# Two pairs of sum banks per layer norm, and half of the last scaling moved to VectorE, in a two-block transformer kernel

## The chip, the cores and the metric

The kernel runs on one core of one Trainium2 chip. The metric is the device time of one execution in microseconds (us). TensorE (PE) does the matmuls, VectorE (DVE) and ScalarE (ACT) the elementwise work, GpSimd (POOL) a few subtractions, and SyncE (SP) issues the DMAs. Each engine works through its own list of instructions in the built program, and waits at one until the results that it needs are there.

## The reference

The model has two blocks over 512 tokens of width 1024. The first (adaptive norm, neighbourhood attention, a spatial gate, a mixture of experts) is not touched by the change. The second has two layers of FFN, mixer, FFN, and each of these six phases ends in a layer norm over the features:

```python
def _layernorm_2(x, g, b):
    xf = x.astype(jnp.float32)
    mu = jnp.mean(xf, axis=-1, keepdims=True)
    var = jnp.mean(jnp.square(xf - mu), axis=-1, keepdims=True)
    return ((xf - mu) * lax.rsqrt(var + LN_EPS)).astype(x.dtype) * g + b

for l in range(DEPTH_2):
    h = 0.5 * _swiglu(x, ffn_w_gate[l, 0], ffn_w_up[l, 0], ffn_w_down[l, 0])
    x = _layernorm_2(ALPHA * x + h, ln_g[l, 0], ln_b[l, 0])
    h = _mixer(x, ...)
    x = _layernorm_2(ALPHA * x + h, ln_g[l, 1], ln_b[l, 1])
    h = 0.5 * _swiglu(x, ffn_w_gate[l, 1], ffn_w_up[l, 1], ffn_w_down[l, 1])
    x = _layernorm_2(ALPHA * x + h, ln_g[l, 2], ln_b[l, 2])
```

## The kernel before, in words

**Layout.** The activations lie transposed: 128 partitions by 8 feature tiles (`d`, 0 to 7) by 512 tokens. Every matmul of the second block is done as three (`mm3`, lines 194 to 196): weights and activations are split into a high part (`wh`, `xh`) and a rest (`wl`, `xl`), and the products high by rest, rest by high and high by high are added in one PSUM bank.

**The six phases.** `second` (line 1483) runs FFN, mixer, FFN, FFN, mixer, FFN; here they and their norms are numbered 1 to 6. Eight PSUM banks are shared out once: six under the tag `any`, two under the tag `yo0`, which only the mixer's output uses. An FFN's output tile is called `y`, a mixer's `yo`; `ft` is the first thing that a phase computes (`first_tiles`, line 1139): four output tiles from the whole input, tokens 0 to 255 first and then tokens 256 to 511, 96 matmuls of 256 columns for each half. `t` is what an FFN computes after them.

**The norm.** The last output tile of an FFN, and the last four of a mixer, are computed in two halves of 256 tokens, so that the norm of the first half can run while TensorE still works on the second. For each tile, `Norm.sums` (line 1080) adds the residual (`x<-x,y`, L1083, VectorE), adds into `S` (L1088, VectorE), squares into `q` (L1090, ScalarE) and adds `q` into `Q` (L1091, VectorE). `Norm.finish` (line 1093) then runs once for each half: `token_stats` (line 1128) sums `S` and `Q` over the partitions by two matmuls with a matrix of ones, into the banks `pS` and `pQ`; ScalarE takes the mean (`mu<-pS`, L1133); VectorE and ScalarE make the variance (L1134, L1135) and its inverse root (L226, L209 to L212), which is written back into `pQ`. For each feature tile VectorE then subtracts the mean (L1117, which reads `pS`) and multiplies by the root (L1118, which reads `pQ`), ScalarE scales and shifts into `x` (L1119) and `xh` (L1124), and GpSimd makes `xl` (L1125). The `ft` matmuls of the next phase read `xh` and `xl`.

**The last norm** has no next phase: ScalarE's L1119 is the last step, and each of its results goes out by a DMA that SyncE issues (L1121). For its second half the mean is subtracted ahead of time (L1108) and VectorE only multiplies (L1115).

**What sets the order.** The kernel is written in one sequence, and a scheduler gives each engine its list when the program is built. A block under `high_priority(offset=150)` is treated as if it had been written 150 instructions earlier, as far as its inputs and its buffers allow; the sums and statistics of the second half of every norm are under it. Both halves of a norm used the same two banks `pS` and `pQ`, so the scheduler had to place the second half's two matmuls behind the first half's L1117 and L1118, which read those banks.

Of the kernel before, what the change touches and what calls it, by code (L numbers as in the profile page):

```python
# [10 lines left out]
AF = mybir.ActivationFunctionType  # L11
OP = mybir.AluOpType
# [17 lines left out]
HALVES = (slice(0, 256), slice(256, 512))  # L30
# [211 lines left out]
def at(xs, k):  # L242
    return xs[k // 4][:, k % 4]
# [79 lines left out]
def first_attention(c, x, cst, v_dram, sums_dram, ada_dram):  # L323

    nc, tc, a = c.nc, c.tc, c.a
    with ExitStack() as st:
# [49 lines left out]
        def heads(w, xh, xl, n, gain, done):  # L376

            ps = [c.ps("ph") for _ in range(2)]
            for k in range(KD):
                for mm in range(2):  # L380
                    c.mm3(ps[mm][:, :n], *w.cols((mm * 8 + k) * P, P), xh(k), xl(k), k == 0, k == 7)
            finish()
            sq = [c.t("hsq") for _ in range(2)]
            for mm in range(2):
                nc.scalar.square(sq[mm][:, :n], ps[mm][:, :n])
            late.append((ps, sq, n, gain, done))
# [40 lines left out]
        for i in range(4):  # L427
            v = c.t("v")
            nc.scalar.copy(v, own(w, i))
            finish()  # L430
            nc.gpsimd.dma_start(v_dram[i * P:(i + 1) * P, :], v)
# [637 lines left out]
class Norm:  # L1069
# [23 lines left out]
    def finish(self, sl):  # L1093
        c, nc, x = self.c, self.c.nc, self.x
        last = self.nxt is None
        steps = []
        if self.out is None:
            self.mu, self.var, self.ps = c.t("mu"), c.t("var"), (c.ps("pS"), c.ps("pQ"))
            self.out = (c.new_xs("xh"), c.new_xs("xl")) if not last else ()
            if not last:  # L1100
                self.w, steps = c.first_chunks(self.nxt, self.early)
        mu, total, rs = self.mu[:, sl], self.ps[0][:, sl], self.ps[1][:, sl]
        with c.tc.high_priority(offset=150 if sl == HALVES[1] else 0):
            token_stats(c, self.S[:, sl], self.Q[:, sl], D, mu, self.var[:, sl], rs, total, rs)
        g, b = (c.v2[:, o + self.col * KD:] for o in (V_LNG, V_LNB))
        if last and sl == HALVES[1]:
            for d in range(KD):
                nc.vector.tensor_sub(x[:, d, sl], x[:, d, sl], mu)  # L1108
        for d in range(KD):
            if steps and d >= 2 * (self.early - 1) and d % 2 == 0:  # L1110
                steps.pop(0)()
            t = c.t("n")[:, sl]
            r = x[:, d, sl]
            if last and sl == HALVES[1]:
                nc.vector.tensor_mul(t, r, rs)  # L1115
            else:
                nc.vector.scalar_tensor_tensor(t, total, -1.0 / D, r, op0=OP.mult, op1=OP.add)  # L1117
                nc.vector.tensor_mul(t, t, rs)  # L1118
            nc.scalar.activation(r, t, AF.Identity, bias=b[:, d:d + 1], scale=g[:, d:d + 1])  # L1119
            if last:  # L1120
                nc.sync.dma_start(c.a["o"][:, d, sl], r)  # L1121
            else:
                h = at(self.out[0], d)[:, sl]
                nc.scalar.activation(h, t, AF.Identity, bias=b[:, d:d + 1], scale=g[:, d:d + 1])  # L1124
                nc.gpsimd.tensor_sub(at(self.out[1], d)[:, sl], r, h.bitcast(F32))  # L1125


def token_stats(c, s, q, n, mu, var, rs, pS, pQ):

    nc = c.nc  # L1130
    nc.tensor.matmul(pS, c.ones, s, start=True, stop=True)
    nc.tensor.matmul(pQ, c.ones, q, start=True, stop=True)
    nc.scalar.mul(mu, pS, 1.0 / n)  # L1133
    nc.vector.tensor_mul(var, mu, mu)  # L1134
    nc.vector.scalar_tensor_tensor(var, pQ, 1.0 / n, var, op0=OP.mult, op1=OP.subtract)  # L1135
    c.rstd(rs, var, 1, 1e-5)
# [488 lines left out]
```

## Time and profile before

| | us |
|---|---|
| time, median of 3 executions | 2525.66 (2525.14 to 2526.16) |
| time of the profiled execution | 2528.47 |
| span of its trace, first to last instruction | 2526.7 |
| TensorE busy | 2417.3 |
| VectorE busy | 1380.8 |
| ScalarE busy | 1070.5 |
| GpSimd busy | 151.7 |
| mean granted TensorE clock | 0.983 |

The profiled execution is 2.81 us above the median, and its trace covers all of it but 1.8 us. Busy times are sums over the span; matmuls overlap one another, and their ends are modelled, so the distance between the starts of neighbouring matmuls tells more than their lengths. In a timeline the columns are the start, the length from the first to the last of a group, the engine, the line, the operation, output<-inputs, the shape and the count; in brackets stands the idle time of the engine just before, and what ended it.

### The profile page before, as it was taken

Reading aid. Unit: us, or ns where it says so; the run is one execution under the profiler, and the core shown is the slowest. Engines: PE = TensorE matmul, PEld = TensorE weight load, DVE = VectorE, ACT = ScalarE, POOL = GpSimd, SP = SyncE. Lnnn points to the kernel's source line nnn. Section 1 sums busy time; section 2 is a strip of 40 time slices with the busy share of each in tenths; the row PEclk is TensorE's granted clock in tenths of the full one; section 3 lists DMA queues with packets and bytes.
Section 4 is the critical chain, followed back from the end, with each engine's and each line's share of the span. In section 5 each row is a group of like instructions: output and inputs, shape, how many; then the busy total and the mean of one; then the engine's idle time right before and its main releaser. Section 6 shows DMA issues by size and latency. Waiting matters only on the chain.

```text
span 2526.7 us, 30984 instructions
## 1 busy us (share of the span) xinstructions
PE 2417.3 (96%) x12289; PEld 1997.4 (79%) x12289; DVE 1380.8 (55%) x2299; ACT 1070.5 (42%) x1646; POOL 151.7 (6%) x187
## 2 busy tenths in 40 slices
PE   7998869999999999998999999999999999999997
PEld 4785558888798888886888888888888867888886
DVE  4836569999733333489833333533333798433334
ACT  4426427888532232356632222522222555522223
POOL 0011101121000000010100000100000200100000
PEclk9999879999999999999999999999999999999999
DMA  7145759999522222321132222222223211222231
GB/s 284 71 125 194 293 218 351 388 394 391 200 82 98 88 94 92 118 100 51 51 109 91 101 92 92 101 100 93 91 95 105 105 67 51 100 88 96 92 98 61
DMA packets 59652, 348.11 MB, mean 138 GB/s; under 512 B 8832, under 2 KB 11104, under 8 KB 23408
## 3 DMA queue, kind: packets, MB, share of 16 engines
q1 hardware_dynamic: 47776, 311.45, 33.5%
q0 software_dynamic: 10576, 32.00, 4.3%
q10 hardware_dynamic: 1152, 2.66, 0.3%
q8 instruction: 97, 1.59, 0.3%
q14 instruction: 51, 0.42, 0.0%
HBM read 329.73 MB, written 16.33 MB: 137 GB/s over the span
## 4 chain that ended last, share of the span: by engine, by line
PE 69%; DVE 7%; issue 5%; ACT 3%; DMA 0%; POOL 0%; SPq 0%; ACTq 0%; another core or an unknown queue 0%; POOLq 0%; DVEq 0%
PE t L194 12%; PE t L195 12%; PE t L196 12%; PE y L194 6%; PE y L196 6%; PE y L195 6%; PE e L194 2%; PE e L196 2%; PE e L195 2%; DVE acc L1256 2%; PE ft L195 1%; PE ft L196 1%; PE ft L194 1%; ACT x L1119 1%; DVE wl L186 1%
## 5 line engine op out<-in xcount | busy, mean ns | idle before, releaser
L185 ACT CAST wh<-raw 128x1024 fp32r<-128x1024 f32 (+1 forms) x504 | 521.5, 1038 | 1069.5 <-PE t L196 364.4
L186 DVE TENSOR_TENSOR wl<-raw,wh 128x1024 fp32r<-128x1024 f32 (+1 forms) x504 | 600.5, 1205 | 624.8 <-ACT wh L185 621.0
L194 PE MATMUL t<-xh,wl 128*128 128x512 f32 x1440 | 561.5, 390 | 0.0
L195 PE MATMUL t<-xl,wh 128*128 128x512 f32 x1440 | 560.6, 389 | 0.0
L196 PE MATMUL t<-xh,wh 128*128 128x512 f32 x1440 | 560.3, 389 | 0.0
L194 PEld LDWEIGHTS t<-xh,wl 128*128 128x128 f32 x1440 | 270.3, 188 | 58.2 <-issue 2.3
L195 PEld LDWEIGHTS t<-xl,wh 128*128 128x128 f32 x1440 | 270.4, 188 | 56.4 <-issue 0.8
L196 PEld LDWEIGHTS t<-xh,wh 128*128 128x128 f32 x1440 | 270.3, 188 | 56.2
L194 PE MATMUL y<-hh,wl 128*128 128x512 f32 (+1 forms) x792 | 289.8, 366 | 2.1 <-DVE x L1083 2.1
L195 PE MATMUL y<-hl,wh 128*128 128x512 f32 (+1 forms) x792 | 290.2, 366 | 0.0
L196 PE MATMUL y<-hh,wh 128*128 128x512 f32 (+1 forms) x792 | 289.4, 365 | 0.0
L1169 DVE SCALAR_TENSOR_TENSOR s<-s,t 128x512 f32<-128x512 f32 x80 | 55.0, 687 | 255.5 <-PE t L196 255.5
L194 PEld LDWEIGHTS y<-hh,wl 128*128 128x128 f32 x792 | 149.3, 189 | 27.1 <-DVE x L1083 2.9
L195 PEld LDWEIGHTS y<-hl,wh 128*128 128x128 f32 x792 | 149.4, 189 | 24.4
L196 PEld LDWEIGHTS y<-hh,wh 128*128 128x128 f32 x792 | 149.4, 189 | 23.9
L1125 POOL TENSOR_TENSOR xl<-x,xh 128x256 fp32r<-128x256 f32 x80 | 62.9, 789 | 1423.6 <-ACT xh L1124 1422.2
L195 PE MATMUL ft<-xl,wh 128*128 128x256 f32 x384 | 109.7, 288 | 3.4 <-POOL xl L1125 3.4
L194 PE MATMUL ft<-xh,wl 128*128 128x256 f32 x384 | 106.0, 286 | 4.8 <-ACT xh L1124 4.8
L194 PE MATMUL e<-wh,hTl 128*128 128x512 f32 x272 | 108.6, 399 | 0.5 <-DVE hTl L186 0.5
L196 PE MATMUL ft<-xh,wh 128*128 128x256 f32 x384 | 108.3, 285 | 0.0
L196 PE MATMUL e<-wh,hTh 128*128 128x512 f32 x272 | 106.9, 393 | 0.0
L195 PE MATMUL e<-wl,hTh 128*128 128x512 f32 x272 | 106.6, 392 | 0.0
(471 smaller groups left out, 3420.4 us busy)
## 6 DMA issues: line engine op xcount, KB each, us to landing
raw<-in_w_gu SPq DMA_DIRECT2D x88, 1024.0 KB, 4.8
raw<-in_w SPq DMA_DIRECT2D x82, 1024.0 KB, 12.0
raw<-in_w_d SPq DMA_DIRECT2D x32, 1024.0 KB, 5.0
raw<-in_w_ada SPq DMA_DIRECT2D x24, 1024.0 KB, 6.7
pair<-in_w SPq DMA_DIRECT2D x14, 1024.0 KB, 11.1
raw<-in_w_in SPq DMA_DIRECT2D x14, 1024.0 KB, 4.8
raw<-in_w_out SPq DMA_DIRECT2D x12, 1024.0 KB, 4.7
raw<-in_w_d SPq DMA_DIRECT2D x32, 384.0 KB, 3.1
```

Source lines behind the costliest of these rows:

```text
L185: self.nc.scalar.copy(h, x)
L186: self.nc.vector.tensor_sub(l, x, h.bitcast(F32))
L194: mm(ps, al, bh, start=first, stop=False)
L195: mm(ps, ah, bl, start=False, stop=False)
L196: mm(ps, ah, bh, start=False, stop=last)
L1119: nc.scalar.activation(r, t, AF.Identity, bias=b[:, d:d + 1], scale=g[:, d:d + 1])
L1125: nc.gpsimd.tensor_sub(at(self.out[1], d)[:, sl], r, h.bitcast(F32))
L1169: nc.vector.scalar_tensor_tensor(s, s, 0.5, ps[1], op0=OP.mult, op1=OP.mult)
L1256: nc.vector.scalar_tensor_tensor(acc[:, t], yp[:, t, j:j + S], w, acc[:, t], op0=OP.mult, op1=OP.add)
```

## The change

Two things change, both in `Norm.finish`. The two sums of a half are no longer slices of one shared pair of banks: the first half takes two banks of the tag `yo0`, the second half takes `pS` and `pQ` from the tag `any`. And in the second half of the last norm the scaling of the odd feature tiles is a VectorE instruction in place of a ScalarE one.

```diff
         if self.out is None:
-            self.mu, self.var, self.ps = c.t("mu"), c.t("var"), (c.ps("pS"), c.ps("pQ"))
+            self.mu, self.var = c.t("mu"), c.t("var")
...
-        mu, total, rs = self.mu[:, sl], self.ps[0][:, sl], self.ps[1][:, sl]
+        mu = self.mu[:, sl]
+        total, rs = (c.ps("yo0" if sl == HALVES[0] else n)[:, sl] for n in ("pS", "pQ"))
         with c.tc.high_priority(offset=150 if sl == HALVES[1] else 0):
             token_stats(c, self.S[:, sl], self.Q[:, sl], D, mu, self.var[:, sl], rs, total, rs)
...
-            nc.scalar.activation(r, t, AF.Identity, bias=b[:, d:d + 1], scale=g[:, d:d + 1])
+            if last and sl == HALVES[1] and d % 2:
+                nc.vector.tensor_scalar(r, t, g[:, d:d + 1], b[:, d:d + 1], op0=OP.mult, op1=OP.add)
+            else:
+                nc.scalar.activation(r, t, AF.Identity, bias=b[:, d:d + 1], scale=g[:, d:d + 1])
```

Line numbers shift: L1108, L1115, L1117 and L1118 become L1109, L1116, L1118 and L1119; from L1119 on it is four (L1119 becomes L1123, L1124 becomes L1128, and the statistics L1131 to L1135 become L1135 to L1139). L1121 is now the new VectorE instruction.

The scheduler makes new lists from this. **First place: TensorE at the end of phase 1**, where the second half's sums stand among the matmuls of phase 2. Before, `pS` came after 32 of the `ft` matmuls and `pQ` after 37 of the 192:

```order
L194 MATMUL ft<-xh,wl 128x256
L195 MATMUL ft<-xl,wh 128x256
L1131 MATMUL pS<-S,consts 128x256
L196 MATMUL ft<-xh,wh 128x256
L194 MATMUL ft<-xh,wl 128x256
L195 MATMUL ft<-xl,wh 128x256
L196 MATMUL ft<-xh,wh 128x256
L194 MATMUL ft<-xh,wl 128x256
L1132 MATMUL pQ<-Q,consts 128x256
L195 MATMUL ft<-xl,wh 128x256
```

and now:

```order
L194 MATMUL y<-hh_6469,wl 128x256
L195 MATMUL y<-hl_6491,wh 128x256
L196 MATMUL y<-hh_6469,wh 128x256
L1135 MATMUL pS<-S,consts 128x256
L1136 MATMUL pQ<-Q,consts 128x256
L194 MATMUL ft<-xh,wl 128x256
L195 MATMUL ft<-xl,wh 128x256
L196 MATMUL ft<-xh,wh 128x256
```

Both sums moved up to just behind the last `y` matmul, ahead of every `ft`. It is the same at the ends of phases 2 to 5, where `pQ` had stood behind 67, 53, 37 and 67 of the `ft` matmuls. At the end of phase 6 there is no `ft`, and TensorE's order is unchanged.

**Second place: VectorE and ScalarE at the same norm**, between the second half's `S` and its `Q`. VectorE before (`n` is the tile being normed, of the first half; `wl` the rest of a weight chunk):

```order
L1088 TENSOR_TENSOR S<-S,x_6300 128x256
L1118 TENSOR_TENSOR n<-n,pQ 128x256
L1117 SCALAR_TENSOR_TENSOR n<-pS,x_6300 128x256 x2
L1118 TENSOR_TENSOR n<-n,pQ 128x256
L186 TENSOR_TENSOR wl<-raw,wh 128x1024
L1118 TENSOR_TENSOR n<-n,pQ 128x256
L1117 SCALAR_TENSOR_TENSOR n<-pS,x_6300 128x256 x2
L1118 TENSOR_TENSOR n<-n,pQ 128x256
L1091 TENSOR_TENSOR Q<-Q,q 128x256
```

and now, with ScalarE's piece behind it:

```order
L1088 TENSOR_TENSOR S<-S,x_6300 128x256
L1119 TENSOR_TENSOR n<-n,yo_8717 128x256
L1118 SCALAR_TENSOR_TENSOR n<-yo_8716,x_6300 128x256 x2
L1119 TENSOR_TENSOR n<-n,yo_8717 128x256
L186 TENSOR_TENSOR wl<-raw,wh 128x1024
L1138 TENSOR_TENSOR var<-mu 128x256
L1119 TENSOR_TENSOR n<-n,yo_8717 128x256
L1118 SCALAR_TENSOR_TENSOR n<-yo_8716,x_6300 128x256 x2
L1119 TENSOR_TENSOR n<-n,yo_8717 128x256
L1091 TENSOR_TENSOR Q<-Q,q 128x256
```

```order
L185 CAST wh<-raw 128x1024
L1137 ACTIVATE mu<-pS 128x256
L1123 ACTIVATE x_6300<-n,vecs_85 128x256
L1128 ACTIVATE xh<-n,vecs_85 128x256
L1123 ACTIVATE x_6300<-n,vecs_85 128x256
L1128 ACTIVATE xh<-n,vecs_85 128x256
L1123 ACTIVATE x_6300<-n,vecs_85 128x256
L1090 ACTIVATE q<-x_6300 128x256
```

On VectorE `var<-mu` of the second half moved up, ahead of `Q`; on ScalarE `mu<-pS` moved up: it had stood behind `q` with two instructions between, and now stands ahead of `q` with five between. `Q` kept its place behind the first half's norm work. In norms 2 and 5 the same moves are made around four `q` and four `Q`, one for each of the mixer's last four tiles.

**Third place: VectorE at the very end.** Before, eight multiplications L1115 ended its list. Now:

```order
L212 TENSOR_TENSOR pQ<-rs_19725,rs_19726 128x256
L1109 TENSOR_TENSOR x_6300<-x_6300,mu 128x256
L1116 TENSOR_TENSOR n<-x_6300,pQ 128x256 x3
L1121 TENSOR_SCALAR x_6300<-n,vecs_85 128x256
L1116 TENSOR_TENSOR n<-x_6300,pQ 128x256 x2
L1121 TENSOR_SCALAR x_6300<-n,vecs_85 128x256
L1116 TENSOR_TENSOR n<-x_6300,pQ 128x256 x2
L1121 TENSOR_SCALAR x_6300<-n,vecs_85 128x256
L1116 TENSOR_TENSOR n<-x_6300,pQ 128x256
L1121 TENSOR_SCALAR x_6300<-n,vecs_85 128x256
```

The four scalings of the odd tiles stand between the multiplications, and one subtraction of the mean moved down behind L212. The lists of GpSimd and SyncE are unchanged.

## Rows read from the trace of the kernel before

**Rows 1.** The page's busy times: engine, busy us (share of the span), instructions.

```profile
PE 2417.3 (96%) x12289; PEld 1997.4 (79%) x12289; DVE 1380.8 (55%) x2299; ACT 1070.5 (42%) x1646; POOL 151.7 (6%) x187
```

**Rows 2.** TensorE's waits from 700 us on: us in total, times, longest us.

```profile
PE ft L194 <- ACT xh L1124: 4.8, 3, 2.1
...
PE pS L1131 <- DVE n L1117: 2.9, 3, 1.9
```

**Rows 3.** Timeline at norm 1 and the ft matmuls behind it, three engines.

```profile
1067.36 0.28 PE L196 MATMUL y<-hh,wh 128*128 128x256 f32 x1
...
1073.28 0.42 DVE L1091 TENSOR_TENSOR Q<-Q,q 128x256 f32<-128x256 f32 x1
...
1074.10 0.70 PE L1132 MATMUL pQ<-Q,consts 128*128 128x256 f32 x2
...
1074.14 0.36 ACT L1133 ACTIVATE mu<-pS 128x256 f32<-128x256 f32 x1
...
1074.44 0.47 PE L195 MATMUL ft<-xl,wh 128*128 128x256 f32 x1
...
1091.76 0.28 PE L195 MATMUL ft<-xl,wh 128*128 128x256 f32 x1
...
1093.68 0.28 PE L196 MATMUL ft<-xh,wh 128*128 128x256 f32 x1
1093.80 0.40 PE L194 MATMUL t<-xh,wl 128*128 128x512 f32 x1
```

**Rows 4.** Timeline at norm 2 (ScalarE's squares, then TensorE's first t).

```profile
1244.06 0.71 ACT L1090 ACTIVATE q<-x 128x256 f32<-128x256 f32 x2
...
1246.45 0.42 ACT L1090 ACTIVATE q<-x 128x256 f32<-128x256 f32 x1 [1.19 <-PE pS L1131]
...
1266.51 0.40 PE L194 MATMUL t<-xh,wl 128*128 128x512 f32 x1
```

**Rows 5.** Timeline at norm 3 (Q, first t), and the first t behind norms 4 and 5.

```profile
1612.12 0.42 DVE L1091 TENSOR_TENSOR Q<-Q,q 128x256 f32<-128x256 f32 x1 [0.23 <-ACT q L1090]
...
1632.44 0.40 PE L194 MATMUL t<-xh,wl 128*128 128x512 f32 x1
...
1998.56 0.40 PE L194 MATMUL t<-xh,wl 128*128 128x512 f32 x1
...
2171.22 0.40 PE L194 MATMUL t<-xh,wl 128*128 128x512 f32 x1
```

**Rows 6.** Stretches: us and PE busy, PEld, DVE, ACT, POOL, PEclk, DMA, GB/s.

```profile
1185.30:1188.70 3.40, 1.34 (x8) 0.70 (x9) 3.37 (x10) 2.05 (x9) 0.00 (x0) 1.00 0.21 89
1188.70:1192.10 3.40, 3.40 (x11) 2.02 (x11) 2.27 (x5) 2.59 (x5) 0.00 (x0) 0.50 0.00 0
1067.00:1075.00 8.00, 7.06 (x51) 6.27 (x50) 7.74 (x22) 8.00 (x18) 6.01 (x10) 1.00 0.88 343
```

**Rows 7.** TensorE's timeline around 386.5 us, where the granted clock rises from 0.50.

```profile
383.14 0.63 PE L196 MATMUL e<-wh,hTh 128*128 128x512 f32 x1
...
385.70 0.63 PE L196 MATMUL e<-wh,hTh 128*128 128x512 f32 x1
...
386.79 0.40 PE L196 MATMUL e<-wh,hTh 128*128 128x512 f32 x1
...
387.95 0.39 PE L195 MATMUL e<-wl,hTh 128*128 128x512 f32 x1
```

**Rows 8.** Timeline of the last norm's second half.

```profile
2511.96 0.42 DVE L1088 TENSOR_TENSOR S<-S,x 128x256 f32<-128x256 f32 x1
...
2513.10 0.70 PE L1131 MATMUL pS<-S,consts 128*128 128x256 f32 x2 [1.92 <-DVE n L1117]
...
2518.06 0.28 DVE L211 TENSOR_SCALAR rs<-rs 128x256 f32<-128x256 f32 x1
...
2519.06 2.74 DVE L1115 TENSOR_TENSOR n<-x,pQ 128x256 f32<-128x256 f32 x8
2519.51 4.04 ACT L1119 ACTIVATE x<-n,vecs 128x256 f32<-128x256 f32 x8 [3.00 <-DVE n L1115]
```

## The prediction

> **What bounds the kernel now.** I read the page's busy times first: TensorE is busy for 96% of the span [rows 1], so what it loses in one place it gets back nowhere else. The next view is what TensorE waits for in the second block [rows 2]: the second half of a phase's `ft` matmuls waits 4.8 us in all for `xh`, and the second half's sum `pS` waits 2.9 us for the first half's L1117, which reads the same bank. Last I read the timeline at the norms. At norm 1 the last `y` matmul starts at 1067.36, `Q` of the second half is added at 1073.28, `pQ` starts at 1074.10, and the first `t` matmul, behind all 192 of `ft`, at 1093.80 [rows 3]. The reader is to see that `Q` comes 6 us after the last `y`, and that TensorE did `ft` work nearly all that time: it is busy for 7.06 of the 8 us from 1067 [rows 6].
>
> **The change part by part.** *The stall at norms 1 to 5.* In the new order `pS` and `pQ` stand ahead of every `ft` matmul, while `Q` kept its place on VectorE behind the first half's norm work. So the whole `ft` now waits for `Q`. I work out when `ft` starts, add its length, and compare with where `t` started.
>
> Length of `ft`: between 1091.76 and 1093.68 lie 16 steps [rows 3], 0.12 us each; 192 of them take 23.04 us. By then its inputs are all there or come faster than they are used, so I add no gaps.
>
> Norm 1: `Q` ended at 1073.28 + 0.42 = 1073.70 [rows 3]. Two instructions moved ahead of it, `var<-mu` on VectorE (one of eight such 256-column rows takes 2.74 / 8 = 0.34 [rows 8]) and `mu` on ScalarE (0.36 [rows 3]); they are on two engines, so I count one of them, 0.3. `Q` then ends at 1074.00. `pQ` starts 0.05 later, and the next matmul 0.34 after that, as it did before (1074.10 to 1074.44 [rows 3]): `ft` starts at 1074.4 and ends at 1097.4. Before, `t` started at 1093.80: **3.6 us** later.
>
> Norm 3: `Q` ended at 1612.12 + 0.42 = 1612.54 [rows 5]; by the same steps `ft` starts at 1613.2 and ends at 1636.3, against 1632.44 [rows 5]: **3.8 us**.
>
> Norm 2: four `q` must be squared. Before, the third waited 1.19 us for `pS` [rows 4], which now comes early, so this wait goes. The four start 0.33 later than 1244.06 and take 3 x 0.31 + 0.41 us (two took 0.71 [rows 4]): done at 1245.7, the last `Q` (0.42) at 1246.2, `ft` from 1246.6 to 1269.6, against 1266.51 [rows 4]: **3.1 us**.
>
> Norms 4 and 5 have the same order as 1 and 2, and their `t` stands 904.76 and 904.71 us behind those [rows 3 to 5]: **3.6 and 3.1 us**. Sum: 17.2 us. An error of 0.5 us in each start of `ft` makes the bounds 14.7 and 19.7. I see nothing that takes it up later: behind `ft` an FFN is all TensorE, and a mixer's VectorE chain starts from the results of `ft`.
>
> *The clock after the stall.* From 1067.4 to 1074.4 TensorE would have nothing but two short sums to do; at norm 2 the wait is longer still. The trace of before has no such hole at a norm (granted clock 1.00 there [rows 6]), but it has them elsewhere: in a stretch with 1.34 us of work in 3.40 the granted clock was still 1.00, and in the next, which was full, it was 0.50, that is 1.2 in place of 2.4 GHz [rows 6]. What that costs: at 0.50 six matmuls of 512 columns take 385.70 - 383.14 = 2.56 us, 0.427 each; at full clock five take 387.95 - 386.79 = 1.16 us, 0.232 each [rows 7]. So 3.4 us of dense work at 0.50 lose 3.4 x (1 - 0.232 / 0.427) = 1.55 us. Part of the slow stretch will lie inside the wait and cost nothing; on the other side it can last for two such stretches. Bounds for each norm: 0 and 3.1 us. I take 1.25, four fifths of one stretch, since the work is dense from the first `ft` on: 5 x 1.25 = **6.2 us**, with 0 and 15.5 as ends.
>
> The Trainium skill (TensorE: Matmul & The Clock Gate, section "HAM oscillation — how this bites in real kernels") says that when TensorE idles between bursts of matmuls its clock is halved, and that every burst then starts cold. By that rule all five norms would pay a whole stretch, an estimated 7.8 us in place of 6.2, and the sum would be 1.6 us higher; the rows agree as far as they go, with the 0.50 right behind the thin stretch [rows 6].
>
> *The tail, norm 6.* TensorE has no `ft` there. `S` was done at 2511.96 + 0.42 = 2512.38, but `pS` started at 2513.10, held by L1117 [rows 8]: 0.7 us of wait go. VectorE has the same work to do up to its first multiplication, so I count half, 0.35 us. Then ScalarE did eight scalings in 4.04 us from 2519.51, 4.5 us after the multiplications began at 2519.06 [rows 8]. Now VectorE does eight multiplications (2.74 us) and four scalings; nearest row: a tensor-scalar of the same shape takes 0.28 [rows 8], at most the 0.42 of a two-tensor one. The last result is there after 2.74 + 4 x 0.28 = 3.9 us, or 4.4 at the upper price: 0.6 or 0.1 sooner. I take the 0.6, since that row has one tensor as input as the new one has. ScalarE's four end earlier. The DMAs are issued as the results come and just move along. Together **1.0 us** sooner, with 0.4 and 1.6 (all of the 0.7 us, and overlap) as ends.
>
> *What costs nothing.* Two more banks are taken only where `yo0` is idle: an FFN does not use it, and the mixer's `yo` tiles in it are read before the norm's first half is summed. The second half's own chain starts a little earlier, but its `xh` are then waited for by nobody, since `ft` itself is late.
>
> Sum: 17.2 + 6.2 - 1.0 = **22.4 us slower**. The rows are from an execution of 2528.47 us, which would become 2550.9; from the median of 2525.66 the forecast is **2548.1 us**.
>
> **The rivals.** *The stall without the clock.* If the two sums in the wait, or its place, keep the clock at 1.00, 17.2 - 1.0 = 16.2 remain: 2541.9. For it: not every thin stretch need be followed by a slow one. Against it: the waits are longer than the thin stretch of [rows 6], and emptier.
>
> *The banks do what they look like (faster).* If `Q` of the second half were done when TensorE reaches `pQ`, the early statistics would bring the second half's `xh` early: the waits of 4.8 us [rows 2] and the 2.9 - 1.92 = 1.0 us for `pS` at norms 1 and 4 [rows 2, 8] would go, with the tail 6.8 us: 2518.9. It decides at one point, whether `Q` ends before the last `y` at 1067.4; it ended at 1073.7 [rows 3], and nothing in the change hurries it.
>
> *Only the tail (no change).* If the stalls were taken up by slack that I don't see, behind `ft` for instance, 1.0 us remains: 2524.7. At 96% busy [rows 1] there is little slack.
>
> **How the numbers follow.** A measurement of this kernel tells 0.2%, 5.05 us, from no change. Chances: stall with slow clock 0.80, stall without it 0.11, only the tail 0.05, faster 0.04. Slower is 0.91, same 0.05, faster 0.04. The range leaves out the last two: from 14.7 + 0 - 1.6 = 13.1 (2538.8) at the low end, to 19.7 + 11 - 0.4 = 30.3 (2556) at the high one, where 11 stands for two slow stretches at about two norms of five; I round outwards, 2537 to 2557.
>
> **What would show it.** Right: at norms 1 to 5 TensorE is nearly idle for 7 to 8 us behind the last `y` or `yo`, waiting at `pQ` for VectorE's `Q` (about 4 us in each, and 1 to 2 at `pS` for `S`); the first `t` stands 3 to 6 us further from the last `y` than before; the granted clock shows 0.50 behind the waits. In the tail `pS` follows `S` at once, and the last output is issued about 1 us sooner after the last `y`. Wrong: `ft` starts before `Q`, or the time behind the last `y` grows by under 2 us, or the clock stays at 1.00 at all five.

## The result, and the profile after

The changed kernel takes 2551.99 us (median of 5 executions, 2550.59 to 2556.09), the kernel before 2526.16 beside it (5 executions, 2525.14 to 2531.03). The ratio is 1.0109, 95% interval 1.0095 to 1.0124: 24 to 31 us, about 1.1%, **slower**. The forecast was 2548.1, range 2537 to 2557, slower with a chance of 0.91: the direction, the place and the mechanism came out; its stall and its clock were too small, and the gain at its end was too large.

The profiled execution of the changed kernel took 2553.06 us; its span is 2551.2, against 2526.7 before, and its mean granted clock 0.977 against 0.983. The page's busy times after, to be held against [rows 1]:

```profile
PE 2422.1 (95%) x12289; PEld 2004.0 (79%) x12289; DVE 1383.7 (54%) x2303; ACT 1069.7 (42%) x1642; POOL 150.1 (6%) x187
```

Little is to be seen there: TensorE gained 4.8 us of busy time and the span 24.5, so most of the loss is waiting. The view that shows it is what TensorE waits for, from 700 us on (us in total, times, longest us):

```profile
PE pQ L1136 <- DVE Q L1091: 26.4, 6, 6.5
...
PE pS L1135 <- DVE S L1088: 8.0, 6, 1.4
```

Both rows are new. The two of [rows 2] are gone: no `ft` waits for `xh` any more (nor for `xl`, 3.4 us before), and `pS` no longer waits for the first half's subtraction. Two waits of 7.7 us were given up for two of 34.4. The timeline at norm 1, TensorE, which answers to [rows 3]:

```profile
1062.57 0.28 PE L196 MATMUL y<-hh,wh 128*128 128x256 f32 x1
1064.29 0.70 PE L1135 MATMUL pS<-S,consts 128*128 128x256 f32 x2 [1.44 <-DVE S L1088]
1069.23 1.22 PE L1136 MATMUL pQ<-Q,consts 128*128 128x256 f32 x2 [4.25 <-DVE Q L1091]
1069.89 0.78 PE L194 MATMUL ft<-xh,wl 128*128 128x256 f32 x1
...
1095.41 0.40 PE L194 MATMUL t<-xh,wl 128*128 128x512 f32 x1
```

Before, `ft` started 0.25 us behind the last `y`; now 7.3 us behind it, with only the two sums in between (x2: the trace has two records for each of them). From the last `y` to the first `t` is 32.84 us; it was 26.44. The next view cuts the same norm into three stretches (us and PE busy, PEld, DVE, ACT, POOL, PEclk, DMA, GB/s):

```profile
1062.70:1069.90 7.20, 1.52 (x7) 0.88 (x5) 7.01 (x17) 7.20 (x16) 5.92 (x10) 0.89 0.87 338
1069.90:1075.10 5.20, 5.20 (x25) 5.11 (x24) 4.12 (x17) 3.49 (x6) 1.58 (x3) 0.50 0.31 129
1075.10:1095.40 20.30, 20.30 (x171) 20.30 (x170) 7.62 (x15) 11.58 (x20) 5.91 (x8) 1.00 0.12 33
```

In the wait TensorE is busy for 1.52 of 7.2 us; in the 5.2 us behind it the granted clock is 0.50 (1.2 GHz) although TensorE is full, and 25 matmuls are done in the time in which 43 would start at the 0.12 us of a dense step; then it is 1.00 again. Before, the clock was 1.00 in this place [rows 6].

**Where the time went.** From the last `y` (or `yo`) to the first `t`, in us, from the timelines; the kernels E1 to E12 are those of the next section:

| kernel | norm 1 | 2 | 3 | 4 | 5 | sum, against before |
|---|---|---|---|---|---|---|
| before | 26.44 | 27.89 | 26.25 | 26.43 | 27.87 | 134.88 |
| after | 32.84 | 34.47 | 32.39 | 32.39 | 33.67 | +30.9 |
| E1 banks only | 31.82 | 34.93 | 32.65 | 32.53 | 34.30 | +31.4 |
| E2 scaling only | 26.44 | 29.38 | 26.26 | 26.43 | 29.39 | +3.0 |
| E3 dummies in the wait | 30.23 | 32.29 | 30.23 | 30.23 | 32.30 | +20.4 |
| E4 order only | 31.84 | 34.53 | 32.59 | 32.48 | 33.54 | +30.1 |
| E5 a bank for S only | 26.33 | 27.20 | 25.95 | 26.37 | 27.19 | -1.8 |
| E6 late sums | 29.09 | 30.11 | 29.22 | 29.08 | 30.11 | +12.7 |
| E7 early Q | 28.42 | 27.57 | 26.50 | 29.72 | 27.59 | +4.9 |
| E8 early Q, shared banks | 31.72 | 30.82 | 29.37 | 30.10 | 30.91 | +18.0 |
| E9 late sums, priority | 26.90 | 28.35 | 26.68 | 26.86 | 29.85 | +3.8 |
| E10 early Q, priority | 27.58 | 28.09 | 25.63 | 27.43 | 28.07 | +1.9 |
| E11 last norm only | 26.45 | 29.38 | 26.26 | 26.43 | 29.37 | +3.0 |
| E12 S bank, last norm both | 26.34 | 27.19 | 25.96 | 26.35 | 27.21 | -1.8 |

The five norms grew by 30.9 us and the stretch behind the last `y` of the kernel shrank by 0.35 (15.76 to 15.42), 30.5 in all. The span grew by only 24.5, because two stretches that the change does not touch were shorter in this one execution: the first block by 4.8 us (the second block's first `ft` at 699.72, before at 704.51) and one mixer by 1.2, at the place of [rows 6] where the clock fell to 0.50 before and stayed at 1.00 here. Both are chance: over the 14 profiles of this study that first `ft` lies between 694.63 and 706.83, whatever the kernel. A span is therefore no measure for a few us here; the table above and the ratios are.

### The profile page after: what moved, and what is told of

The parts are those of the page before. It is cut to its first block, busy times and chain, and to the rows that moved or that the text cites. A ratio compares the mean times of both kernels' runs of the same rounds, so it can differ in the third digit from the quotient of the medians.

```text
span 2551.2 us, 30981 instructions
## 1 busy us (share of the span) xinstructions
PE 2422.1 (95%) x12289; PEld 2004.0 (79%) x12289; DVE 1383.7 (54%) x2303; ACT 1069.7 (42%) x1642; POOL 150.1 (6%) x187
## 4 chain that ended last, share of the span: by engine, by line
PE 75%; DVE 6%; ACT 3%; issue 1%; DMA 0%; DVEq 0%; another core or an unknown queue 0%; ACTq 0%; SPq 0%
PE t L194 12%; PE t L195 12%; PE t L196 12%; PE y L194 7%; PE y L196 7%; PE y L195 7%; PE e L194 2%; PE e L196 2%; PE e L195 2%; PE ft L194 2%; PE ft L195 2%; PE ft L196 2%; DVE acc L1260 2%; ACT wh L185 1%; DVE wl L186 1%
## 5 line engine op out<-in xcount | busy, mean ns | idle before, releaser
L194 PE MATMUL ft<-xh,wl 128*128 128x256 f32 x384 | 114.7, 299 | 0.0
## 6 DMA issues: line engine op xcount, KB each, us to landing
pair<-in_w SPq DMA_DIRECT2D x14, 1024.0 KB, 11.6
```

Of the source, the lines that this page charges most:

```text
L194: mm(ps, al, bh, start=first, stop=False)
```

## The experiments

All are compared with runs of the kernel before on the same chip, five rounds each. **E1 and E2 split the change** into its two parts: the banks, and the scaling on VectorE.

```diff
 E1, from the changed kernel:
-            if last and sl == HALVES[1] and d % 2:
-                nc.vector.tensor_scalar(r, t, g[:, d:d + 1], b[:, d:d + 1], op0=OP.mult, op1=OP.add)
-            else:
...
+            nc.scalar.activation(r, t, AF.Identity, bias=b[:, d:d + 1], scale=g[:, d:d + 1])
 E2, from the changed kernel:
-            self.mu, self.var = c.t("mu"), c.t("var")
+            self.mu, self.var, self.ps = c.t("mu"), c.t("var"), (c.ps("pS"), c.ps("pQ"))
...
-        mu = self.mu[:, sl]
-        total, rs = (c.ps("yo0" if sl == HALVES[0] else n)[:, sl] for n in ("pS", "pQ"))
+        mu, total, rs = self.mu[:, sl], self.ps[0][:, sl], self.ps[1][:, sl]
```

> The changed kernel with only its banks: all scalings of the last norm are back on ScalarE. TensorE's list is that of the changed kernel, with both sums of the second half ahead of every ft at norms 1 to 5. Theory (the stall behind the two sums, and the half clock that follows it, are the whole loss): about 2552 us, within 3 us of the changed kernel; from the last y to the first t 32 to 35 us at each of norms 1 to 5, as in the changed kernel. Rival (the four scalings on VectorE cost something, or pay more than the tail showed): the time moves by over 3 us from 2552.

> The kernel before with only the other part of the change: the shared banks stay, and VectorE scales the odd tiles of the last norm's second half. Theory: only the end of the kernel moves, by the 0.35 us that the changed kernel's tail gained or less: 2525 to 2526.5 us, no difference that the times can tell; norms 1 to 5 as before, 26 to 28 us from the last y to the first t. Rival (the scaling carries part of the loss): over 2529.

Measured: E1 2549.66 us, ratio 1.0092 (1.0074 to 1.0109); E2 2522.43, ratio 0.9992 (0.9981 to 1.0002). The banks are the whole loss, and the scaling is not told from nothing (the 2522.43 lies below the range that I had named, but the kernel before took 2524.47 beside it). That the norms of E2 are not quite those of before (29.38 at norms 2 and 5) has one cause, the clock of that execution, since TensorE's list is the same; the stretch in E2, columns as above:

```profile
1252.82:1256.20 3.38, 3.38 (x18) 3.38 (x18) 0.54 (x2) 3.38 (x8) 2.55 (x4) 0.50 0.02 5
```

It costs 1.49 us at each of the two norms. E11 shows the same. So the sum of the kernel before, which had no such stretch in its one profile, may be some 3 us on the low side as a yardstick; the last column of the table would then be 3 us too high in every row below it.

**E3 parts the stall from the clock.** Dummy matmuls fill the wait; their result is overwritten by the real sum, so the output does not change.

```diff
 def token_stats(...):
     nc.tensor.matmul(pS, c.ones, s, start=True, stop=True)
+    for _ in range(fill):   # second half of norms 1 to 5: 13 behind a mixer, 8 behind an FFN
+        nc.tensor.matmul(pQ, c.ones, c.k[:, C_ONE:C_ONE + 256], start=True, stop=True)
     nc.tensor.matmul(pQ, c.ones, q, start=True, stop=True)
```

> The changed kernel with dummy matmuls of 256 columns (ones by constants, overwritten by the real sum) between the second half's pS and pQ at norms 1 to 5: eight behind an FFN, thirteen behind a mixer, about as long as the wait for Q. ft still waits for Q, so the stall stays; only the emptiness of TensorE goes. Theory (the clock is a cost of its own): the granted clock stays at 1.00 through norms 1 to 5, the 192 ft take 23.0 to 23.3 us in place of 24.3 to 25.5, the matmul pQ 0.34 us in place of 0.66, and the kernel is 8 to 12 us faster than the changed one: 2540 to 2544. If the dummies run past Q they delay ft by up to 1 us a norm, 2545 to 2549. Rival (the half clock lies where it costs nothing): 2552, ft as long as in the changed kernel.

Measured: 2541.85 us, ratio 1.0063 (1.0047 to 1.0078), in the range of the theory; the rival's 2552 is out. The timeline of E3 at norm 1, TensorE (x16: two records for each of the eight dummies):

```profile
1067.53 0.70 PE L1136 MATMUL pS<-S,consts 128*128 128x256 f32 x2 [1.43 <-DVE S L1088]
1068.06 3.62 PE L1138 MATMUL pQ<-consts 128*128 128x256 f32 x16
1072.48 0.70 PE L1139 MATMUL pQ<-Q,consts 128*128 128x256 f32 x2 [0.80 <-DVE Q L1091]
1072.83 0.47 PE L194 MATMUL ft<-xh,wl 128*128 128x256 f32 x1
```

and the stretches of E3 from the last `y` to the first `ft` and from there to the first `t`:

```profile
1065.90:1072.80 6.90, 4.67 (x22) 3.63 (x20) 6.70 (x17) 6.90 (x15) 5.57 (x10) 1.00 0.91 335
1072.80:1096.00 23.20, 23.20 (x194) 23.17 (x193) 12.20 (x31) 15.29 (x27) 7.86 (x11) 1.00 0.18 65
```

`ft` waits as long as in the changed kernel (7.0 us behind the last `y`; the 0.3 that are missing are `pQ` itself, 0.35 to `ft` in place of 0.66), but the clock stays at 1.00 at all five norms and the 192 `ft` take 23.22 us, where the changed kernel took 25.52, 25.10, 25.06, 25.07 and 24.29. Work that computes nothing made the changed kernel faster. So of the 30.9 us 20.4 are the stall and 10.5 the clock: 8.9 in `ft`, 1.6 in `pQ`. The times agree on the clock (E3 is 10.1 us below the changed kernel), but put E3 only 12 to 20 us above the kernel before, where the traces say 20.4 less the 0.35 of the tail; with the 3 us of the yardstick taken off it is 17.

**E4 parts the order from the banks**: the kernel before, its two shared banks untouched, with the first 12 `ft` matmuls (and by their order all) held behind the second half's `pQ`.

```diff
-    nc.tensor.matmul(pQ, c.ones, q, start=True, stop=True)
+    c.sums = nc.tensor.matmul(pQ, c.ones, q, start=True, stop=True)
...
+                if c.sums and sl == HALVES[0] and k == 0:
+                    for m in three:   # the three matmuls of mm3
+                        c.queue(m, c.sums)
```

> The kernel before, with its two shared banks, and only TensorE's order that of the changed kernel: every ft is held behind the second half's pQ. Theory (the order is what costs, not the banks): norms 1 to 5 look like the changed kernel's, 31.5 to 35 us from the last y to the first t, granted clock 0.50 behind the waits, 2550 to 2555 us in all; mu and var stand behind Q as in the kernel before, so Q may end 0.3 us sooner at each norm. Rival (the two banks under the tag yo0 are themselves the cost, for instance by holding up the first half or the mixer's output): about 2526.

Measured: 2554.15 us, ratio 1.0110 (1.0092 to 1.0127), the theory. What TensorE waits for in E4:

```profile
PE pS L1131 <- DVE n L1117: 28.2, 6, 5.4
...
PE pQ L1132 <- DVE Q L1091: 3.3, 2, 1.6
```

With shared banks the same time is lost at `pS`, for the first half's L1117, and hardly at `pQ` for `Q` (26.4 there in the changed kernel). The names of the wait changed; the loss did not. So the separate banks cost nothing by themselves: they only took away what had kept the two sums back in TensorE's list.

**E5: only S has a bank of its own for each half**, so that `pS` stands ahead of every `ft`, and `pQ` behind 41 or 56.

```diff
-        total, rs = (c.ps("yo0" if sl == HALVES[0] else n)[:, sl] for n in ("pS", "pQ"))
+        if sl == HALVES[0]:
+            self.ps = c.ps("yo0"), c.ps("pQ")
+        else:
+            self.ps = c.ps("pS"), self.ps[1]
+        total, rs = (p[:, sl] for p in self.ps)
```

> Only the sum S gets a bank of its own for each half; both halves still share the bank of Q. In the built order pS of the second half then stands ahead of every ft at norms 1 to 5, but pQ behind 41 or 56 of them. Theory (what a wait ahead of ft costs is only what outlasts the later wait for the second half's xh): ft starts about 2.0 us behind the last y in place of 0.2, but the second half's xh come no later than before, and the kernel before waited for them; so y to t stays within 1 us of the 26 to 28 us of the kernel before, the clock stays at 1.00, and the time is 2522 to 2529, no difference that the times tell. Rival (every microsecond that ft waits is lost): 1.8 us at each of five norms, and the clock may fall too: 2533 or more.

Measured: 2523.16 us, ratio 0.9985 (0.9973 to 0.9996): the theory. TensorE's waits in E5:

```profile
PE pS L1139 <- DVE S L1088: 8.0, 6, 1.4
...
PE ft L194 <- ACT xh L1132: 1.8, 2, 0.9
```

`pS` waits the same 8.0 us as in the changed kernel, with all of `ft` behind it, and the norms are 1.8 us shorter than before. At norm 1 `ft` starts at 1066.01, 2.07 us behind the last `y` where it was 0.25, and `t` comes 0.11 sooner. The time is taken from the later wait for the second half's `xh` (4.8 us before [rows 2], 1.8 here), and those for `xl` fell from 3.4 to 1.2 as well. A wait ahead of `ft` costs only what outlasts the wait that comes later anyway.

**E6 to E10 ask whether the separate banks can pay** if the sums stand better. In E6 the statistics of the second half are written among the next phase's `ft`, without the priority of 150 places.

```diff
-        with c.tc.high_priority(offset=150 if sl == HALVES[1] else 0):
+        with c.tc.high_priority(offset=150 if sl == HALVES[1] and last else 0):
...
 def first_tiles(c, w, xh, xl, norm=None):   # norm.behind: 5 behind a mixer, 4 behind an FFN
...
+            if norm and sl == HALVES[0] and k + 1 == norm.behind:
+                norm.finish(HALVES[1])
```

> The changed kernel, banks and all, with the second half's statistics of norms 1 to 5 written among the next phase's ft (behind 48 or 60 of its 192 matmuls), so that the sums stand there in TensorE's list and not ahead of ft. Theory (the stall came from the place in the order alone): no wait for Q of over 1 us, granted clock 1.00, y to t at most the 26.3 to 27.9 us of the kernel before: 2521 to 2526 us, about 27 faster than the changed kernel and not told from the one before. Rival (the separate banks cost something wherever the sums stand): 2530 or more.

Measured: 2533.97 us, ratio 1.0033 (1.0020 to 1.0046). Faster than the changed kernel by 18 us, and still slower than before: the theory as I had put it fell, since I had counted the place of the two matmuls alone. The time lies in the range of the rival, whose reason E9 takes away. What TensorE waits for in E6 (`ft` for `xh`; 4.8 before):

```profile
PE ft L194 <- ACT xh L1129: 11.4, 5, 2.7
```

The stall was gone from the front of `ft` and stood in its middle, and behind this wait the clock fell as well, at all five norms; at norm 1:

```profile
1078.13:1081.54 3.41, 3.41 (x15) 3.22 (x16) 2.09 (x7) 3.26 (x7) 2.65 (x4) 0.50 0.00 0
```

E9 keeps the two matmuls there and gives the steps behind them (mean, variance, root) their priority back.

```diff
+    with c.tc.high_priority(offset=hurry):   # 150 for the second half of norms 1 to 5
         nc.scalar.mul(mu, pS, 1.0 / n)
...
         c.rstd(rs, var, 1, 1e-5)
```

> The kernel with the sums written late, and the steps behind the second half's sums (mean, variance, inverse root) given back the priority of 150 places that they have in the kernel before; the two sum matmuls stay behind 16 to 69 of ft. Theory (the 1.2 to 3.0 us by which the version without that priority lengthened y to t came from this: the root stood behind the first half's x and xh on ScalarE, so the second half's xh came late): y to t back to 25.5 to 28 us, 2521 to 2528. Rival (separate banks cost something wherever the sums stand): y to t stays at 29 to 30 us, 2531 to 2536.

Measured: 2527.79 us, ratio 1.0011 (1.0001 to 1.0021); `ft` waits 7.3 us for `xh`. The theory holds for most of it: four norms are at 26.7 to 28.4 us (I had said 28 at most), and the fifth had a stretch at clock 0.50. Each of those four remains 0.43 to 0.46 us longer than before.

E7 has Q early: five of the first half's eight tiles are written behind the second half's sums, and the statistics are written behind 24 or 36 of `ft` (in the trace the sums stand behind 16 to 36). E8 is the same with shared banks, E10 with the priority of E9.

```diff
 E7, from E6:
-                if d == KD - 1 and (sl == HALVES[0] or nxt is None):
-                    norm.finish(sl)
+                elif d == KD - 1 and sl == HALVES[0]:
+                    norm.stats(sl)
+                    norm.tiles(sl, range(3))
+                elif d == KD - 1:
+                    norm.tiles(HALVES[0], range(3, KD))
 E8, from E7:
-        total, rs = (c.ps("yo0" if sl == HALVES[0] else n)[:, sl] for n in ("pS", "pQ"))
+        if sl == HALVES[0]:
+            self.ps = c.ps("pS"), c.ps("pQ")
+        total, rs = (p[:, sl] for p in self.ps)
```

> The kernel of the run before, with the second half's q and Q made early: only three feature tiles of the first half's norm are written ahead of the second half's sums, the other five behind them, and the statistics behind 24 or 36 of ft. Q then stands five multiplications earlier on VectorE, and q behind three tiles on ScalarE. Theory (the separate banks are worth something once Q is early; before, the second half's xh came late because Q came late): y to t falls to 24.3 to 25.5 us at norms 1, 3 and 4 and to 24.5 to 26.5 at 2 and 5, 5 to 11 us in all: 2514 to 2520. Rival (the first half's xh, now behind q and mu on ScalarE, starve the first ft as much as the second half gains): 2523 to 2527.

> The same early Q, but both halves share the two banks as in the kernel before. The scheduler then puts the second half's pS and pQ behind the first half's last subtraction and multiplication again: behind 36 to 55 ft matmuls, 16 to 31 more than with the separate banks at the norms, some 2 to 3.5 us later. Theory (bank and early Q are worth something only together): y to t lies between, at 25 to 27 us, and the time at 2518 to 2524, 3 to 6 us above the version with the separate banks. Rival (the early Q alone brings the gain): the same time as with separate banks, within 2 us.

> The kernel with the early q and Q, again with the priority of 150 places for the steps behind the second half's sums. Theory (an early Q is worth something if the chain behind it is early too): the root and the second half's first xh come 2 to 3 us sooner than without that priority; y to t at 24.5 to 26.5 us at the five norms, 2513 to 2522, below both kernels. Rival (what the second half gains the first half's x and xh lose on ScalarE, and ft waits for those): 2523 to 2528.

Measured: E7 2527.53, ratio 1.0005 (0.9994 to 1.0015); E8 2542.53, ratio 1.0062 (1.0047 to 1.0077); E10 2525.08, ratio 0.9995 (0.9985 to 1.0005). The gains that I had expected of E7 and E10 did not come, although `Q` of the second half was done 4.2 us behind the last `y` at norm 1 of either, where it had been 6.35. The reason shows for one part: in E10 `ft` waits only 1.5 us for `xh` (4.8 before), but 5.8 us for `xl`, which GpSimd makes behind `x` and `xh` (3.4 before). In E10:

```profile
PE ft L195 <- POOL xl L1141: 5.8, 13, 1.0
PE pQ L1148 <- DVE Q L1093: 1.8, 3, 0.7
...
PE ft L194 <- ACT xh L1140: 1.5, 4, 0.5
```

That is the rival I had named, in the form that the first `ft` lose what the later ones gain. These waits sum to less than before, while the norms are 1.9 us longer. Measured from start to start at the five norms, TensorE's steps that end in one of these waits last 12.1 us beyond dense steps in E10 and 11.6 before; the other 1.4 us are in steps too short for that view to name what they waited for, and their cause stays open. E8 against E7 shows that the separate banks can be worth something: with the same early Q, shared banks are 15 us slower, more than the 3 to 6 that I had expected, because the sums then wait for the first half's subtraction (up to 2.2 us) and a stretch at clock 0.50 follows in each of the five norms of E8, and in one of E7.

**E11 and E12 look at what could be kept.** E11 is the change in the last norm alone; E12 is E5 with separate banks for both sums in the last norm.

```diff
 E11, from the changed kernel:
-        total, rs = (c.ps("yo0" if sl == HALVES[0] else n)[:, sl] for n in ("pS", "pQ"))
+        if sl == HALVES[0] or last:
+            self.ps = [c.ps("yo0" if sl == HALVES[0] and last else n) for n in ("pS", "pQ")]
+        total, rs = (p[:, sl] for p in self.ps)
 E12, from E5:
-            self.ps = c.ps("yo0"), c.ps("pQ")
+            self.ps = c.ps("yo0"), c.ps("yo0" if last else "pQ")
...
-            self.ps = c.ps("pS"), self.ps[1]
+            self.ps = c.ps("pS"), c.ps("pQ") if last else self.ps[1]
```

> The change in the last norm alone, banks and VectorE scaling; norms 1 to 5 share their two banks as before, and TensorE's list is that of the kernel before. Theory: only the end moves, by what the changed kernel's tail showed: the last output 12.2 to 12.4 us behind the last y in place of 12.7, 2523 to 2526, no difference that the times tell. Rival (the tail is worth the 1 us of the forecast): the last output at 11.7 or less.

> What the runs so far leave as the best of the change: at norms 1 to 5 only S has a bank of its own for each half and pQ shares one as before, so that only pS stands ahead of ft; in the last norm both sums have their own banks, and VectorE scales the odd tiles. Theory (both parts hold, they are small): y to t within 0.2 us of the 26.33, 27.20, 25.95, 26.37 and 27.19 of the version with S's bank alone, 1.8 us less in all than the kernel before, the last output 12.3 us behind the last y unless pQ runs at half clock there; 2521 to 2525, its interval against the kernel before below 1.000. Rival (the small gain of the version with S's bank alone was chance): the interval holds 1.000.

Measured: E11 2521.78, ratio 0.9990 (0.9979 to 1.0000); E12 2522.89, ratio 0.9994 (0.9983 to 1.0005). E11 lies 1.2 us below the range that I had named, beside a kernel before at 2524.82. In E12 the norms repeat those of E5 to 0.02 us, so the 1.8 us there are real in the traces; its ratio holds 1.000, so the times don't confirm a gain over the kernel before. E5, E11 and E12 all beat the changed kernel by some 29 us; against the kernel before, only E5's interval lies below 1.000, and barely. In E11 the last output was issued 12.77 us behind the last `y` in place of 12.2 to 12.4: `pQ` ran slower there (its two records start 0.56 us apart, 0.32 before; 0.59 in E2), and the tail was no shorter than before. In E12 it was issued at 12.61, where I had said 12.3: there the two records start 0.40 apart, so `pQ` was slowed in part.

## Why the prediction was right, and where its terms were off

**The mechanism** held step by step. `pS` followed `S` (1.44 us of wait), `pQ` waited 4.25 us at norm 1 and 6.5 at norm 2, no `ft` started before `Q`, and the clock was 0.50 behind all five waits. The first `t` stood 5.8 to 6.6 us further from the last `y` than before, at and above the top of the 3 to 6 that I had named. E1 and E2 put all of it on the banks, E4 on the order that they set free, E3 on the two terms.

**The stall: 17.2 forecast, 20.4 measured** (E3's trace against the one trace of before, from which the forecast was made; the times put E3's whole loss at 12 to 20 us, which bears out 17.2 better than 20.4). The start of `ft` was right at the FFN norms: I had put `Q` 0.3 us later behind the last `y` than before, and it ended 6.61 us behind it in place of 6.35. Two steps were small. I took `ft` at 23.04 us from an extrapolated step of 0.12; dense, it took 23.22, 0.9 in all. And at norms 2 and 5 `Q` came 1.07 us later than I said, 2.1 in all: the step that failed is that I let the last `Q` follow the last `q` at once. VectorE at norm 2 of the changed kernel:

```profile
1244.93 0.42 DVE L1119 TENSOR_TENSOR n<-n,yo 128x256 f32<-128x256 f32 x1
1245.27 2.39 DVE L1091 TENSOR_TENSOR Q<-Q,q 128x256 f32<-128x256 f32 x4
```

The squares were done at 1246.09, as forecast, but the four additions, each of which needs the one before, started 0.53 us apart, the last of them took 0.81 us in place of 0.42 (no run here shows why), and they ended at 1247.66.

**The clock: 6.2 forecast, 10.5 measured.** The step that failed is "four fifths of one stretch" of 3.4 us for each norm. 4.2 to 5.2 us of `ft` ran at half clock at norms 1 to 4, since the clock rose only well after the work had become dense, and I had left out that `pQ` itself is slowed (0.66 to the next matmul in place of 0.34). My bounds for a norm, 0 and 3.1, held: the parts of `ft` are 1.1 to 2.3, and `pQ` adds 0.3. The rule of the Trainium skill that I had weighed (TensorE: Matmul & The Clock Gate, section "HAM oscillation — how this bites in real kernels"), that every burst behind an idle stretch starts cold, held at all five norms of the changed kernel (0.50 behind each), but not behind the shorter waits of E5, where `ft` starts 2 us behind the last `y` and the clock stayed at 1.00; the 7.8 us that I had estimated by it were nearer than my 6.2, and still too few.

**The tail: 1.0 forecast, 0.35 measured.** Its first half was right: the multiplications began 7.82 us behind the last `y` in place of 8.15, half of the wait of `pS`. Of the second half, 0.6 for the scalings on VectorE, 0.06 was left. VectorE took 4.15 us from its first multiplication to the last result, where I had said 3.9 and ScalarE's last result had come after 4.49. The step that failed is "the DMAs are issued as the results come and just move along". The eight output DMAs of the last half, as SyncE (SPq) issues them, after:

```profile
2544.72 3.76 SPq L1125 DMA_DIRECT2D out<-x  x8
```

and before:

```profile
2520.14 3.78 SPq L1121 DMA_DIRECT2D out<-x  x8
```

Either way they take the same time: in the changed kernel the last result was done 11.97 us behind the last `y` (L1121 at 2547.38 for 0.41), 0.67 sooner than before, and its DMA was issued 0.30 later, since SyncE issues one each 0.49 us and was still behind. ScalarE's results had come at just that pace. E1, with all scalings on ScalarE, issued its last output 0.06 us later than the changed kernel.

**The rivals.** "The stall without the clock", 2541.9, is what E3 made (2541.85), the price of a kernel that was not there; that the two agree to 0.1 us is luck, since E3's trace has 3 us more of stall than that price. "The banks do what they look like" was ill put: I let it decide on whether `Q` ends before the last `y`, which it never can, since `Q` takes in the square of that very tile. What decides is how much of the wait for `Q` is filled by `ft` ahead of `pQ`, and the most that any of these kernels gained at the five norms is E5's 1.8 us. "Only the tail" fell.

**The sum.** 20.4 + 10.5 - 0.35 = 30.5 against 22.4; the ratio gives 24 to 31, with 27.5 in the middle, which is the 30.5 less the 3 us of the yardstick. From one profile to another the chance shifts named above hid 6.0 us of it; had I read the spans alone I would have called my sum nearly exact.

## What to carry to other kernels

A false dependency can be holding an instruction in a good place: before it is taken away (here by a second pair of banks), look where the scheduler puts the freed instruction in an in-order list, and what it will wait for there. A wait on the busiest engine costs what outlasts the next wait behind it, so 1.4 us at `pS` were free and 4 to 6.5 at `pQ` were not; where a wait can't be avoided, matmuls that compute nothing can be worth their place: here the clock stayed at 1.00 with them, and they gave back a third of the loss. And a step moved to another engine pays only if what follows it (here SyncE's issuing) is not just as slow.

## What was not expected of the hardware

- VectorE's four dependent additions `Q<-Q,q` of 128x256 start 0.53 us apart (1245.27, 1245.79, 1246.32, 1246.85), where independent ones of the same shape start 0.33 apart (four L1109 subtractions of the changed kernel in 1.42 us).
- SyncE issued the output DMAs of 128x256 floats 0.49 us apart even where the results were there earlier (0.30 us earlier for the last one).
- The half clock did not end with the wait: at norm 2 of the changed kernel it began 1.9 us after `pS` and lasted 10.2 us, 4.2 of them with dense `ft`. The two stretches, wait and `ft`:

```profile
1242.38:1248.38 6.00, 0.66 (x3) 0.57 (x3) 4.94 (x13) 6.00 (x14) 3.97 (x5) 0.50 0.50 175
1248.38:1252.62 4.24, 4.24 (x21) 4.15 (x20) 2.56 (x8) 2.37 (x4) 0.73 (x1) 0.50 0.00 0
```

- With the dummies in the wait the clock stayed at 1.00 at all five norms (E3), while waits of 2.0 to 2.7 us in the middle of `ft` were each followed by 3.4 us at 0.50 in E6; E2 and E11 had such stretches at norms 2 and 5 with the very list of the kernel before, whose own profile had none. When exactly the clock falls is not settled by these runs.
